# Expert lookup of a two-block network: a kept instruction order for VectorE and ScalarE, and another sharing of the gathered rows

## The chip, the cores and the metric

The kernel runs on one core of a Trainium2 chip. The metric is the device time of one execution in microseconds (us); lower is better. Engines are named as in the profile: PE (TensorE matmuls; PEld is its weight load), DVE (VectorE), ACT (ScalarE), POOL (GpSimd), SP (SyncE, which here only issues transfers).

## The reference

Two network blocks run one after the other on 512 tokens of width 1024 in float32. The change lies in one part of the first block, an expert layer: each token picks 16 of 16384 one-neuron experts for each of 8 heads, and the output is the weighted sum of the experts' rows of v.

```python
def block(xb):
    q = (xb @ wq).reshape(PEER_BLOCK, PEER_HEADS, 2, PEER_DKEY // 2)
    s1 = jnp.einsum('thd,hnd->thn', q[:, :, 0], keys[:, 0]).astype(f32)
    s2 = jnp.einsum('thd,hnd->thn', q[:, :, 1], keys[:, 1]).astype(f32)
    v1, i1 = lax.top_k(s1, PEER_TOPK)
    v2, i2 = lax.top_k(s2, PEER_TOPK)
    cand = (v1[..., :, None] + v2[..., None, :]).reshape(PEER_BLOCK, PEER_HEADS, PEER_TOPK * PEER_TOPK)
    sc, ci = lax.top_k(cand, PEER_TOPK)
    e = (jnp.take_along_axis(i1, ci // PEER_TOPK, axis=-1) * PEER_NKEYS
         + jnp.take_along_axis(i2, ci % PEER_TOPK, axis=-1))
    g = jax.nn.softmax(sc, axis=-1)
    hid = jnp.einsum('thkd,td->thk', u[e], xb).astype(f32)
    a = (jax.nn.gelu(hid, approximate=False) * g).astype(xb.dtype)
    return jnp.einsum('thk,thkd->td', a, v[e])
```

## The kernel before

The first 128 tokens gather their experts' rows; the other 384 take all 16384 experts densely and weigh the unchosen ones with zero. The layer runs in four stages, and PE works through all of them.

**Choice, with u sums beside it.** For each block of 128 tokens, `topk_block` picks the experts with chains of short DVE instructions (`top16`), a POOL sum and some one-hot comparisons. Meanwhile PE makes the u sums for the dense tokens: 64 pairs of 128 experts each (`hidden`), every pair in two pieces of weights. A piece comes in by SP as `raw` (512 KB), ACT rounds it to `whi` (L147), DVE makes the rest `wlo` (L149), and PE does 24 matmuls with them (L71, L72 with the high part of x, L76 with the low part). `wget` has the next two pieces split ahead. A finished pair goes through Gelu on ACT to `G` (L1250) and on to memory.

**Rows of u.** As soon as the first block has chosen, `Rows.step` runs among the rest: POOL gathers 128 rows of u (one for each of the first 128 tokens, 512 KB; four buffers), and DVE multiplies and sums them against the tokens (L1026). There are 128 such steps for u and later 128 for v (L1030).

**Build.** After the last choice, `build` makes the dense weights (expert x token), four tokens at a time, 96 groups: DVE writes two one-hot tiles (`hot`, L1208 and L1211), ACT scales one of them (L1210, four instructions), PE multiplies them (`aps`, L1227, two buffers), and ACT copies the result (L1228). They go to memory as `Ad`. The u sums go on beside it.

**v sums.** For each of the 128 blocks of experts: `gt` (the Gelu of the u sums, read back by ACT's queue) times `at` (the dense weights, read back four blocks at a time by POOL's queue, 768 KB, two buffers) on DVE (L1319), split into `ah` (ACT) and `al` (DVE, L289), and 24 matmuls with the block of v, whose weights come as `raw`, `whi` and `wlo` as above, into eight accumulators. About one row of v per block is gathered and added (L1030) among them.

A scheduler fixes the order of the instructions of each engine when the program is built; each engine then runs its list in that order and stops at any instruction whose inputs or buffers aren't ready. Two things in the text steer it. `pace` takes the u sums in quarters of a pair, and after each quarter lets `side` do work worth `SHARE / 2`, counted in the costs `T16`, `T256`, `TLK`, `BUILD` and `ROW`; `UPACE` says how many steps of `Rows` are owed for each unit of the other work. And `keep_in_program_order` pins single instructions behind what was written before them on their engine, among them the transfers of `at`.

Of the kernel before, what the change touches and what calls it, by code (L numbers as in the profile page):

```python
# [10 lines left out]
F32R = mybir.dt.float32r  # L11
U32 = mybir.dt.uint32
AF = mybir.ActivationFunctionType
ALU = mybir.AluOpType
# [4 lines left out]
P = 128  # L19
D = 1024  # L20
KT = 8
# [24 lines left out]
def r32(ap):  # L46
    return ap.bitcast(F32)


def mmx(nc, r, items, start, stop):  # L50


    rh, rl = r
    for out, (lh, ll) in items:
        nc.tensor.matmul(out, lh, rh, start=start, stop=False)  # L55
        nc.tensor.matmul(out, ll, rh, start=False, stop=False)  # L56
    for out, (lh, _) in items:
        nc.tensor.matmul(out, lh, rl, start=False, stop=stop)
# [54 lines left out]
def h_tiles(g):  # L113
    for k in range(KT):
        g.h[k] = g.res.tile([P, T], F32, tag=f"h{k}", name=f"h{k}")
# [7 lines left out]
def wsrc(g, name, idx):  # L123
    a = g.A[name]
    for i in idx:
        a = a[i]
    return a
# [14 lines left out]
def wload(g, raw, pool, hl):  # L142

    nc = g.nc
    _, a, b = raw.shape
    hi = pool.tile([P, a, b], F32R, tag="whi", name="whi", bufs=hl)
    nc.scalar.activation(hi, raw, AF.Copy)  # L147
    lo = pool.tile([P, a, b], F32R, tag="wlo", name="wlo", bufs=hl)
    nc.vector.tensor_tensor(lo, raw, r32(hi), op=ALU.subtract)  # L149
    return hi, lo  # L150
# [136 lines left out]
def split(g, t, hi, lo):  # L287
    g.nc.scalar.activation(hi, t, AF.Copy)  # L288
    g.nc.vector.tensor_tensor(lo, t, r32(hi), op=ALU.subtract)  # L289
# [647 lines left out]
NK = 128  # L937
TOPK = 16
FIRST = 4
LAST = 3  # L940
N1 = 122
PARTS = 4


GT = 128
RG = P // GT
NJ = P // RG
ND = S - GT
UG = 4

CH = 64
NCK = ND // CH

UH = 120

T16, T256, TLK, BUILD, ROW = 1.8, 2.55, 1.6, 1.3, 1.4
TOPKS = 16 * T16 + 3 + 8 * T256 + 8 * TLK + 2
BUILDS = NCK * (0.8 + CH // 4 * BUILD)
UPACE = UH * ROW / (3 * TOPKS + BUILDS)
SHARE = (4 * TOPKS + BUILDS + UH * ROW + 8) / N1  # L960


# [96 lines left out]
def peer_block(g, ni, tail):  # L1059

    tc, nc, A = g.tc, g.nc, g.A
    with ExitStack() as es:
# [7 lines left out]
        order = list(range(NK - FIRST, NK)) + list(range(NK - FIRST))  # L1070
        acc = Acc(g, es, "p_mm", 5).of(S)
        rg = Rows(g, es)
        g.third = rg.p

        with ExitStack() as e1:
# [105 lines left out]
            def tokens_last(b):  # L1181

                lists = picked[b]
                ps = pS.tile([P, 4, NK], F32, tag="S", name="lps")
                for i in range(3):
                    tc.keep_in_program_order(nc.tensor.transpose(ps[:, i], lists[:, i].rearrange("p a b -> p (a b)"), g.ident))
                lt = ip.tile([P, 3, P], F32, name=f"lt{b}")
                nc.scalar.activation(lt, ps[:, 0:3], AF.Copy)
                return lt
# [11 lines left out]
            def onehots(lt, t4):  # L1201

                o1, o2, oh = [hot[i].rearrange("p (t n) -> p t n", n=NK) for i in (t4 % 3, 3 + t4 % 2, 5 + t4 % 3)]

                def each(i):
                    return lt[:, i, 4 * t4:4 * t4 + 4].unsqueeze(2).to_broadcast([P, 4, NK])

                nc.vector.tensor_tensor(o2, io4, each(1), op=ALU.is_equal)  # L1208
                for j in range(4):
                    nc.scalar.activation(oh[:, j], o2[:, j], AF.Copy, scale=lt[:, 2, 4 * t4 + j:4 * t4 + j + 1])  # L1210
                nc.vector.tensor_tensor(o1, io4, each(0), op=ALU.is_equal)  # L1211
                return o1, oh

            def build(ab, c):

                b, t0 = divmod(GT + c * CH, P)
                lt = chosen[b]
                buf = ab.tile([P, NK, CH], F32, tag="ab", name="ab")
                nxt = [onehots(lt, t0 // 4), onehots(lt, t0 // 4 + 1)]
                yield 0.8  # L1220
                for t4 in range(CH // 4):
                    o1, oh = nxt.pop(0)
                    if t4 < CH // 4 - 2:
                        nxt.append(onehots(lt, t0 // 4 + t4 + 2))
                    ps = pA.tile([P, 4, NK], F32, tag="A", name="aps")
                    for j in range(4):
                        nc.tensor.matmul(ps[:, j], o1[:, j], oh[:, j], start=True, stop=True)  # L1227
                    nc.scalar.activation(buf[:, :, 4 * t4:4 * t4 + 4].rearrange("p i t -> p t i"), ps, AF.Copy)  # L1228
                    if out:
                        nc.scalar.dma_start(*out.pop(0))  # L1230
                    yield BUILD
                n = NK // (CH // 4)
                for i in range(0, NK, n):
                    out.append((Ad[c, :, i:i + n], buf[:, i:i + n]))

            def hidden(i, ts=None):

                at = {}

                def step(p):  # L1240
                    if p == 0:
                        at["acc"] = [acc.get(ND) for _ in range(2)]
                        at["gen"] = gemm2(g, [a[0] for a in at["acc"]], "peer_u", i, X)
                    for _ in range(8 // PARTS):
                        next(at["gen"])
                    if p < PARTS - 1:
                        return
                    gt = gp.tile([P, 2, ND], F32, tag="G", name="G") if ts is None else ts
                    for e in range(2):
                        nc.scalar.activation(gt[:, e], at["acc"][e][1], AF.Gelu)  # L1250
                    if ts is None:
                        nc.scalar.dma_start(Gd[i], gt)
                return [(lambda p=p: step(p)) for p in range(PARTS)]

            chosen, picked = {}, {}
            out = []

            def weights():

                for b in range(4):  # L1260
                    for n, c in enumerate(topk_block(b)):
                        yield c
                        if n == 12 and GT < b * P:
                            chosen[b - 1] = tokens_last(b - 1)
                for _ in range(8):
                    yield 1.0
                chosen[3] = tokens_last(3)
                e2.close()
                ab = e1.enter_context(tc.tile_pool(name="p_ab", bufs=2))
                for c in range(NCK):  # L1270
                    yield from build(ab, c)
                while out:
                    tc.keep_in_program_order(nc.gpsimd.dma_start(*out.pop(0)))

            def side():
                owed = 0.0
                for c in weights():
                    yield c
                    if rg.chosen:
                        owed += c * UPACE  # L1280
                        while owed > 0:
                            owed -= ROW
                            rg.step()
                            yield ROW
# [22 lines left out]
        def expert(n):  # L1307
            i = order[n]
            for m in range(n - n % 4, min(n + 5, NK), 4):
                if order[m] not in ats:  # L1310
                    ats[order[m]] = four_in(order[m])
            for m in range(n - n % 2, min(n + 4, NK), 2):
                if order[m] not in gts:
                    gts[order[m]] = two_in(order[m])
            return weighted(ats[i - i % 4][:, :, i % 4], gts[i - i % 2][:, i % 2])

        def weighted(at, gt):
            gv = gt.rearrange("p (c t) -> p c t", t=CH)
            nc.vector.tensor_tensor(gv, gv, at, op=ALU.mult)  # L1319
            ah = lp.tile([P, ND], F32R, tag="ah", name="ah")  # L1320
            al = lp.tile([P, ND], F32R, tag="al", name="al")
            split(g, gt, ah, al)
            return ah, al

        ats[NK - FIRST] = four_in(NK - FIRST)
        for i in range(NK - FIRST, NK, 2):
# [1 line left out]

        for i in range(N1 // 2, NK // 2):
            for m in hidden(i, gts.get(2 * i)):  # L1330
                m()
        h_tiles(g)
        tail.load(es)
        accs = [pp.tile([P, 512], F32, name=f"acc{k}") for k in range(3)] + [acc.get()[1] for _ in range(5)]
        rg.empty(accs, xh[0][:, 0:S])
        rg.due(NK - LAST)
        for n, i in enumerate(order[:-LAST]):
            a = expert(n)
            vh, vl = wget(g, "peer_v", i)
            mmx(nc, a, [(accs[k][:, GT:], (vh[:, k], vl[:, k])) for k in range(KT)], False, False)  # L1340
            rg.steps()
            if 8 <= n < 8 + KT:
                tc.keep_in_program_order(nc.sync.dma_start(g.h[n - 8][:, NM:], Hd[n - 8]))
        g.third = None

        last = [(expert(n), wload(g, wraw(g, wsrc(g, "peer_v", (order[n],))), lp, LAST)) for n in range(NK - LAST, NK)]
        for k in range(KT):
            for j, (a, (vh, vl)) in enumerate(last):
                mm3(nc, accs[k][:, GT:], (vh[:, k], vl[:, k]), a, False, False)
# [904 lines left out]
```

## Time and profile before

| What | Value |
|---|---|
| time, median of 3 runs | 3697.31 us (3693.34 to 3698.88) |
| profiled execution: time, span | 3703.12 us, 3701.4 us |
| mean granted clock of PE | 0.969 of full |
| busy share of the span: PE, DVE, ACT, POOL | 95%, 64%, 43%, 23% |
| rows of u begin, last choice ends | 679 us, about 971 us |
| build ends, v sums begin | 1303 us, 1335 us |
| v sums end, all but the last three blocks | 1943 us |

The span is that of one profiled execution, 1.7 us short of its own time. The busy time of PE is modelled from pipelined instructions, so it is a share of time with matmuls under way, not of peak speed. A granted clock of 1.00 is 2.4 GHz, 0.50 is 1.2 GHz, and a value between them is a mean over the stretch.

### The profile page before, as it was taken

The page shows a single profiled execution, that of the slowest core. Times are in us where ns is not written, and L with a number is a line of the kernel's source. Part 1 is how long each engine was busy: PE and PEld are TensorE (multiplying, and loading weights), DVE is VectorE, ACT ScalarE, POOL GpSimd, SP SyncE. Part 2 cuts the span into 40 slices and gives each one's busy share as a digit, 9 for nine tenths or more (in the row PEclk, how much of TensorE's full clock was granted, in tenths as well). Part 3 has the DMA queues.
Part 4 walks back from the last instruction along what each step waited for, and adds up shares of the span by engine and source line. Part 5 has one row for each costly group of instructions (what it writes and reads, how often), then busy time and mean ns, then how long its engine had stood idle before and what let it go on. Part 6 is the DMA issues. An engine that isn't in the chain of part 4 may idle for free. (4 is left out here: it accounts for less than half of the span.)

```text
span 3701.4 us, 56411 instructions
## 1 busy us (share of the span) xinstructions
PE 3510.0 (95%) x21979; PEld 3205.8 (87%) x21979; DVE 2381.2 (64%) x4395; ACT 1577.5 (43%) x2998; POOL 865.5 (23%) x828
## 2 busy tenths in 40 slices
PE   8999999899898888989989999999999999999999
PEld 6777888898898888889888899999999998877887
DVE  5764458899977756767677667767653336565333
ACT  4555333333498832333236444545432234443222
POOL 2431010444422134334433223222110003110000
PEclk9999999999999999999998889999999999999999
DMA  4223243777777788988882211111122222212232
GB/s 132 80 82 90 86 132 114 237 265 266 265 250 265 247 293 307 314 300 314 300 284 72 65 51 60 52 51 57 46 82 91 92 92 87 73 58 96 92 97 91
DMA packets 169492, 557.60 MB, mean 151 GB/s; under 512 B 19617, under 2 KB 20130, under 8 KB 169224
## 3 DMA queue, kind: packets, MB, share of 16 engines
q1 hardware_dynamic: 90228, 313.50, 25.6%
q0 software_dynamic: 49136, 170.64, 13.9%
q10 hardware_dynamic: 29860, 69.84, 5.3%
q8 instruction: 173, 2.83, 0.3%
q14 instruction: 95, 0.78, 0.1%
HBM read 492.20 MB, written 55.41 MB: 148 GB/s over the span
## 5 line engine op out<-in xcount | busy, mean ns | idle before, releaser
L72 PE MATMUL ps<-xh,wlo 128*128 128x264 f32 (+2 forms) x3296 | 1056.5, 332 | 61.0 <-DVE wlo L149 60.8
L71 PE MATMUL ps<-xh,whi 128*128 128x264 f32 (+2 forms) x3296 | 1073.2, 337 | 17.8 <-ACT xh L288 13.1
L147 ACT ACTIVATE whi<-raw 128x1024 fp32r<-128x1024 f32 x562 | 591.7, 1057 | 1010.2 <-PE ps L76 767.6
L149 DVE TENSOR_TENSOR wlo<-raw,whi 128x1024 fp32r<-128x1024 f32 x562 | 711.8, 1267 | 358.9 <-ACT whi L147 355.9
L76 PE MATMUL ps<-xl,whi 128*128 128x264 f32 (+2 forms) x3296 | 815.2, 332 | 6.6 <-DVE xl L289 6.5
L72 PEld LDWEIGHTS ps<-xh,wlo 128*128 128x128 f32 x3296 | 633.9, 193 | 103.6 <-DVE wlo L149 73.5
L71 PEld LDWEIGHTS ps<-xh,whi 128*128 128x128 f32 x3296 | 634.0, 193 | 55.8 <-ACT xh L288 15.4
L76 PEld LDWEIGHTS ps<-xl,whi 128*128 128x128 f32 x3296 | 566.5, 193 | 39.3 <-DVE xl L289 8.7
L1017 POOL DMA_INDIRECT row<-in_peer_v_dram,rix x128 | 202.1, 1579 | 369.4 <-DVE ro L1030 334.1
L1017 POOL DMA_INDIRECT row<-in_peer_ur_dram,rix x128 | 167.9, 1312 | 403.7 <-DVE row L1026 315.2
L71 PE MATMUL ps<-ah,whi 128*128 128x264 f32 (+1 forms) x768 | 230.1, 320 | 0.0
L72 PE MATMUL ps<-ah,wlo 128*128 128x264 f32 (+1 forms) x768 | 229.9, 320 | 0.0
L55 PE MATMUL ps<-ah,whi 128*128 128x384 f32 x640 | 224.5, 351 | 0.0
L56 PE MATMUL ps<-ah,wlo 128*128 128x384 f32 x640 | 223.4, 349 | 0.0
L288 ACT ACTIVATE ah<-gt 128x384 fp32r<-128x384 f32 x128 | 63.7, 524 | 323.5 <-DVE gt L1319 323.5
L56 PE MATMUL acc<-ah,wlo 128*128 128x384 f32 x384 | 138.6, 361 | 55.0 <-DVE wlo L149 54.8
L1319 DVE TENSOR_TENSOR gt<-gt,at 128x384 f32<-128x384 f32 x128 | 65.8, 553 | 187.3 <-DMA at<-Ad 178.5
L280 POOL TENSOR_TENSOR ssum<-ssum,sq 128x512 f32<-128x512 f32 (+1 forms) x49 | 75.7, 1550 | 456.5 <-ACT sq L279 456.1
L1026 DVE SCALAR_TENSOR_TENSOR row<-row,rx 128x1024 f32<-128x1024 f32 x128 | 168.0, 1313 | 6.6 <-DMA row<-in_peer_ur_dram,rix 6.6
L76 PE MATMUL ps<-al,whi 128*128 128x264 f32 (+1 forms) x768 | 163.2, 321 | 0.0
L1030 DVE SCALAR_TENSOR_TENSOR ro<-row,rhid,ro 128x1024 f32<-128x1024 f32 x127 | 162.4, 1279 | 0.0
L71 PEld LDWEIGHTS ps<-ah,whi 128*128 128x128 f32 x768 | 144.3, 188 | 11.3
(429 smaller groups left out, 6293.4 us busy)
## 6 DMA issues: line engine op xcount, KB each, us to landing
raw<-in_peer_u_dram SPq DMA_DIRECT2D x128, 512.0 KB
raw<-in_peer_v_dram SPq DMA_DIRECT2D x128, 512.0 KB
raw<-in_ff_up_dram SPq DMA_DIRECT2D x64, 512.0 KB
raw<-in_ff_down_dram SPq DMA_DIRECT2D x64, 512.0 KB
at<-Ad POOLq DMA_DIRECT2D x32, 768.0 KB
raw<-in_gdn_in_dram SPq DMA_DIRECT2D x48, 512.0 KB
Gd<-G ACTq DMA_DIRECT2D x62, 384.0 KB
gt<-Gd ACTq DMA_DIRECT2D x62, 384.0 KB
```

The costliest lines, as they stand in the source:

```text
L55: nc.tensor.matmul(out, lh, rh, start=start, stop=False)
L56: nc.tensor.matmul(out, ll, rh, start=False, stop=False)
L71: nc.tensor.matmul(segs[s][0], lh, xh[:, sl], start=start, stop=False)
L72: nc.tensor.matmul(segs[s][0], ll, xh[:, sl], start=False, stop=False)
L76: nc.tensor.matmul(segs[s][0], lh, xl[:, sl], start=False, stop=stop)
L147: nc.scalar.activation(hi, raw, AF.Copy)
L149: nc.vector.tensor_tensor(lo, raw, r32(hi), op=ALU.subtract)
L280: g.nc.gpsimd.tensor_tensor(self.t[:, 0:n], self.t[:, 0:n], sq[:, 0:n], op=ALU.add)
L1017: nc.gpsimd.indirect_dma_start(out=t, out_offset=None, in_=(self.U, self.V)[e], in_offset=bass.IndirectOffsetOnAxis(ap=self.ix[:, j:j + 1] ...
L1026: o = nc.vector.scalar_tensor_tensor(t, t, 1.0, self.x, op0=ALU.mult, op1=ALU.mult, accum_out=a)
L1030: o = nc.vector.scalar_tensor_tensor(self.o, t, a, self.o, op0=ALU.mult, op1=ALU.add)
L1319: nc.vector.tensor_tensor(gv, gv, at, op=ALU.mult)
```

## The change

From the end of the last choice to the end of the v sums, the scheduler no longer orders DVE and ACT: they keep the order in which the text is written (`manual_schedule`). The text is rearranged to suit:

- In the build, the copy of a group's result stands behind the four scalings of a later group (`last`), and the Gelu of a pair behind the first quarter of the next pair (`ends`).
- In the v sums, block n+2 is prepared while block n is multiplied (`AHEAD_V`): its product with `at` and its `ah` ahead of the row step, its `al` behind it.
- The 120 steps on rows of u that `side` hands out are shared as 44 in the choice and 76 in the build, where one pace served both before; and the costs of the choice's parts are set higher.

No instruction of DVE, ACT, PE or a transfer is added or taken away. Lines after L938 move down by 2 to 22.

```diff
+AHEAD_V = 2
...
-UH = 120
-
-T16, T256, TLK, BUILD, ROW = 1.8, 2.55, 1.6, 1.3, 1.4
+UH, UT = 120, 44
+
+T16, T256, TLK, BUILD, ROW = 2.2, 3.1, 2.0, 1.3, 1.4
 TOPKS = 16 * T16 + 3 + 8 * T256 + 8 * TLK + 2
 BUILDS = NCK * (0.8 + CH // 4 * BUILD)
-UPACE = UH * ROW / (3 * TOPKS + BUILDS)
+UPACE = [UT * ROW / (3 * TOPKS + 8), (UH - UT) * ROW / BUILDS]
 SHARE = (4 * TOPKS + BUILDS + UH * ROW + 8) / N1
...
+        kept, order_kept = es.enter_context(ExitStack()), []
...
                 nxt = [onehots(lt, t0 // 4), onehots(lt, t0 // 4 + 1)]
+                last = None
                 yield 0.8
...
-                    nc.scalar.activation(buf[:, :, 4 * t4:4 * t4 + 4].rearrange("p i t -> p t i"), ps, AF.Copy)
+                    if last is not None:
+                        last()
+                    last = lambda t4=t4, ps=ps: nc.scalar.activation(buf[:, :, 4 * t4:4 * t4 + 4].rearrange("p i t -> p t i"), ps, AF.Copy)
                     if out:
                         nc.scalar.dma_start(*out.pop(0))
                     yield BUILD
+                last()
...
                     for _ in range(8 // PARTS):
                         next(at["gen"])
-                    if p < PARTS - 1:
-                        return
+                    if p == 0 and ends:
+                        ends.pop(0)()
+                    if p == PARTS - 1:
+                        ends.append(end)
+
+                def end():
                     gt = gp.tile([P, 2, ND], F32, tag="G", name="G") if ts is None else ts
                     for e in range(2):
                         nc.scalar.activation(gt[:, e], at["acc"][e][1], AF.Gelu)
...
                 chosen[3] = tokens_last(3)
+                order_kept.append(kept.enter_context(tc.manual_schedule(engines={mybir.EngineType.DVE, mybir.EngineType.Activation})))
...
-                        owed += c * UPACE
+                        owed += c * UPACE[len(order_kept)]
...
-        def weighted(at, gt):
+            gt = gts[i - i % 2][:, i % 2]
             gv = gt.rearrange("p (c t) -> p c t", t=CH)
-            nc.vector.tensor_tensor(gv, gv, at, op=ALU.mult)
+            nc.vector.tensor_tensor(gv, gv, ats[i - i % 4][:, :, i % 4], op=ALU.mult)
             ah = lp.tile([P, ND], F32R, tag="ah", name="ah")
-            al = lp.tile([P, ND], F32R, tag="al", name="al")
-            split(g, gt, ah, al)
-            return ah, al
+            nc.scalar.activation(ah, gt, AF.Copy)
+
+            def lo():
+                al = lp.tile([P, ND], F32R, tag="al", name="al")
+                nc.vector.tensor_tensor(al, gt, r32(ah), op=ALU.subtract)
+                return ah, al
+            return lo
...
+        a = [expert(n)() for n in range(AHEAD_V)]
         for n, i in enumerate(order[:-LAST]):
-            a = expert(n)
             vh, vl = wget(g, "peer_v", i)
-            mmx(nc, a, [(accs[k][:, GT:], (vh[:, k], vl[:, k])) for k in range(KT)], False, False)
+            lo = expert(n + AHEAD_V) if n + AHEAD_V < NK else None
+            mmx(nc, a[n], [(accs[k][:, GT:], (vh[:, k], vl[:, k])) for k in range(KT)], False, False)
             rg.steps()
+            if lo is not None:
+                a.append(lo())
...
+        kept.close()
         g.third = None
```

On DVE these counts stand in the built orders (`wlo` pieces, steps on rows of u, one-hot tiles):

| Stretch of DVE's order | before | after |
|---|---|---|
| first choice block, before the first row step | 14 wlo | 15 wlo |
| first row step to the last second-level choice | 59 wlo, 68 rows, 8 hot | 52 wlo, 39 rows, 6 hot |
| from there to the last one-hot tile | 46 wlo, 54 rows, 184 hot | 52 wlo, 79 rows, 186 hot |

In the middle of the v sums DVE had two products of `gt` and `at` in a row, and two `al` in a row, of blocks close to the one that PE was at:

```order
L1319 TENSOR_TENSOR gt<-gt,at 128x384 x2
L149 TENSOR_TENSOR wlo<-raw,whi 128x1024
L1030 SCALAR_TENSOR_TENSOR ro<-row,rhid,ro 128x1024
L289 TENSOR_TENSOR al<-gt,ah 128x384 x2
L149 TENSOR_TENSOR wlo<-raw,whi 128x1024
L1030 SCALAR_TENSOR_TENSOR ro<-row,rhid,ro 128x1024
```

There it has now, for two blocks (`wlo`, `gt` and `al` of block n+2, `ro` in step n):

```order
L149 TENSOR_TENSOR wlo<-raw,whi 128x1024
L1331 TENSOR_TENSOR gt<-gt,at 128x384
L1032 SCALAR_TENSOR_TENSOR ro<-row,rhid,ro 128x1024
L1337 TENSOR_TENSOR al<-gt,ah 128x384
L149 TENSOR_TENSOR wlo<-raw,whi 128x1024
L1331 TENSOR_TENSOR gt<-gt,at 128x384
L1032 SCALAR_TENSOR_TENSOR ro<-row,rhid,ro 128x1024
L1337 TENSOR_TENSOR al<-gt,ah 128x384
```

The product with `at` stands two blocks ahead of PE now, and one block's work is a unit that repeats.

In the middle of the build, DVE's order before, with the tiles of a token block (`lt_8873`) and row steps between them:

```order
L1211 TENSOR_TENSOR hot<-iota,lt_8873 128x512
L149 TENSOR_TENSOR wlo<-raw,whi 128x1024
L1208 TENSOR_TENSOR hot<-iota,lt_8873 128x512
L1211 TENSOR_TENSOR hot<-iota,lt_8873 128x512
L149 TENSOR_TENSOR wlo<-raw,whi 128x1024
L1208 TENSOR_TENSOR hot<-iota,lt_8873 128x512
L1211 TENSOR_TENSOR hot<-iota,lt_8873 128x512
L1208 TENSOR_TENSOR hot<-iota,lt_8873 128x512
```

And at the same place now:

```order
L149 TENSOR_TENSOR wlo<-raw,whi 128x1024
L1212 TENSOR_TENSOR hot<-iota,lt_8611 128x512
L1215 TENSOR_TENSOR hot<-iota,lt_8611 128x512
L1028 SCALAR_TENSOR_TENSOR row,rhid<-row,rx 128x1024
L1212 TENSOR_TENSOR hot<-iota,lt_8611 128x512
L1215 TENSOR_TENSOR hot<-iota,lt_8611 128x512
L1028 SCALAR_TENSOR_TENSOR row,rhid<-row,rx 128x1024
L149 TENSOR_TENSOR wlo<-raw,whi 128x1024
```

A row step stands behind almost every group now, and a piece's `wlo` comes once in two groups.

## Rows read from the trace of the kernel before

**Rows 1.** The page's first part: busy time and share of the span of each engine
```profile
...
PE 3510.0 (95%) x21979; PEld 3205.8 (87%) x21979; DVE 2381.2 (64%) x4395; ACT 1577.5 (43%) x2998; POOL 865.5 (23%) x828
...
```

**Rows 2.** Windows by stage: PE, PEld, DVE, ACT, POOL busy (instructions), PE clock, DMA share, GB/s
```profile
...
679.00:971.00 292.00, 272.00 (x1502) 263.70 (x1502) 288.67 (x797) 102.15 (x151) 125.80 (x79) 0.96 0.80 269
971.00:1303.00 332.00, 296.36 (x1915) 289.40 (x1914) 253.09 (x363) 265.02 (x565) 85.82 (x60) 0.98 0.74 254
1303.00:1335.00 32.00, 22.34 (x116) 19.48 (x114) 8.37 (x9) 9.69 (x15) 14.31 (x26) 0.91 0.85 313
1335.00:1943.00 608.00, 551.34 (x3006) 540.81 (x3006) 421.14 (x516) 189.08 (x256) 229.21 (x159) 0.96 0.87 302
1943.00:3701.40 1758.40, 1706.83 (x12328) 1561.36 (x12328) 1006.86 (x1929) 711.85 (x1422) 269.05 (x335) 0.96 0.23 74
...
```

**Rows 3.** Waits of the v sums, 1335 to 1943: total, times, longest us
```profile
...
DVE gt L1319 <- DMA at<-Ad: 178.5, 30, 7.8
...
PE acc L56 <- DVE wlo L149: 54.8, 24, 4.6
...
```

**Rows 4.** Timeline of one expert group of the v sums: start, us, engine, line
```profile
...
1606.15 1.02 DVE L1319 TENSOR_TENSOR gt<-gt,at 128x384 f32<-128x384 f32 x2
...
1609.12 0.89 POOL L1294 DMA_DIRECT2D at<-Ad  x1
...
1611.49 1.28 DVE L1030 SCALAR_TENSOR_TENSOR ro<-row,rhid,ro 128x1024 f32<-128x1024 f32 x1
...
1613.18 0.19 PEld L55 LDWEIGHTS acc<-ah,whi 128*128 128x128 f32 x1
...
1617.34 0.19 PEld L55 LDWEIGHTS acc<-ah,whi 128*128 128x128 f32 x1
...
1619.99 1.03 DVE L1319 TENSOR_TENSOR gt<-gt,at 128x384 f32<-128x384 f32 x2 [7.22 <-DMA at<-Ad]
...
1620.94 1.22 DVE L149 TENSOR_TENSOR wlo<-raw,whi 128x1024 fp32r<-128x1024 f32 x1
...
1622.07 1.28 DVE L1030 SCALAR_TENSOR_TENSOR ro<-row,rhid,ro 128x1024 f32<-128x1024 f32 x1
1622.20 0.19 PEld L56 LDWEIGHTS acc<-ah,wlo 128*128 128x128 f32 x1 [4.68 <-DVE wlo L149]
...
1623.27 1.02 DVE L289 TENSOR_TENSOR al<-gt,ah 128x384 fp32r<-128x384 f32 x2
...
1624.20 1.22 DVE L149 TENSOR_TENSOR wlo<-raw,whi 128x1024 fp32r<-128x1024 f32 x1
...
```

**Rows 5.** Windows of 5 us in the v sums, columns as in Rows 2
```profile
...
1615.00:1620.00 5.00, 2.85 (x17) 2.53 (x15) 0.01 (x1) 0.00 (x0) 0.00 (x0) 1.00 1.01 383
1620.00:1625.00 5.00, 2.79 (x9) 2.79 (x10) 5.00 (x7) 2.88 (x4) 1.01 (x1) 0.75 0.64 222
...
```

**Rows 6.** Groups of instructions, 679 to 971, shapes apart
```profile
...
L72 PE MATMUL ps<-xh,wlo 128*128 128x384 f32 x472 | 163.8, 347 | 20.0 <-DVE wlo L149 19.9
...
L1026 DVE SCALAR_TENSOR_TENSOR row<-row,rx 128x1024 f32<-128x1024 f32 x68 | 93.9, 1382 | 5.6 <-DMA row<-in_peer_ur_dram,rix 5.6
...
L149 DVE TENSOR_TENSOR wlo<-raw,whi 128x1024 fp32r<-128x1024 f32 x59 | 79.4, 1346 | 0.0
...
```

**Rows 7.** Timeline at the end of the build: matmuls of one group of four tokens
```profile
...
1303.11 1.03 PEld L1227 LDWEIGHTS aps<-hot 128*128 128x128 f32 x8
...
```

**Rows 8.** Groups of instructions, 971 to 1303, shapes apart
```profile
...
L72 PE MATMUL ps<-xh,wlo 128*128 128x384 f32 x384 | 131.4, 351 | 33.8 <-DVE wlo L149 33.7
...
L1228 ACT ACTIVATE ab<-aps 128x512 f32<-128x512 f32 x95 | 102.8, 1083 | 19.4 <-PE aps L1227 17.6 <-issue 1.7
...
L1026 DVE SCALAR_TENSOR_TENSOR row<-row,rx 128x1024 f32<-128x1024 f32 x56 | 69.2, 1236 | 1.0 <-DMA row<-in_peer_ur_dram,rix 1.0
L1211 DVE TENSOR_TENSOR hot<-iota,lt 128x512 f32<-128x512 f32 x93 | 64.2, 690 | 65.5 <-PE aps L1227 64.5 <-issue 0.7
...
L147 ACT ACTIVATE whi<-raw 128x1024 fp32r<-128x1024 f32 x46 | 48.9, 1066 | 18.2 <-PE ps L76 10.9 <-DMA raw<-in_peer_u_dram 7.3
...
```

More of the change, by code (lines that the diff above doesn't have):

```diff
@@ L1253, in hidden @@
                 return [(lambda p=p: step(p)) for p in range(PARTS)]
+            ends = []
             chosen, picked = {}, {}
@@ L1314, in expert @@
                     gts[order[m]] = two_in(order[m])
-            return weighted(ats[i - i % 4][:, :, i % 4], gts[i - i % 2][:, i % 2])
-        def weighted(at, gt):
+            gt = gts[i - i % 2][:, i % 2]
             gv = gt.rearrange("p (c t) -> p c t", t=CH)
-            nc.vector.tensor_tensor(gv, gv, at, op=ALU.mult)
+            nc.vector.tensor_tensor(gv, gv, ats[i - i % 4][:, :, i % 4], op=ALU.mult)
             ah = lp.tile([P, ND], F32R, tag="ah", name="ah")
-            al = lp.tile([P, ND], F32R, tag="al", name="al")
-            split(g, gt, ah, al)
-            return ah, al
+            nc.scalar.activation(ah, gt, AF.Copy)
[4 more added lines that the diff above has]
+            return lo
         ats[NK - FIRST] = four_in(NK - FIRST)
@@ L1331, in peer_block @@
                 m()
+        while ends:
+            ends.pop(0)()
         h_tiles(g)
@@ L1336, in peer_block @@
         rg.due(NK - LAST)
+        a = [expert(n)() for n in range(AHEAD_V)]
         for n, i in enumerate(order[:-LAST]):
-            a = expert(n)
             vh, vl = wget(g, "peer_v", i)
-            mmx(nc, a, [(accs[k][:, GT:], (vh[:, k], vl[:, k])) for k in range(KT)], False, False)
+            lo = expert(n + AHEAD_V) if n + AHEAD_V < NK else None
+            mmx(nc, a[n], [(accs[k][:, GT:], (vh[:, k], vl[:, k])) for k in range(KT)], False, False)
             rg.steps()
+            if lo is not None:
+                a.append(lo())
             if 8 <= n < 8 + KT:
                 tc.keep_in_program_order(nc.sync.dma_start(g.h[n - 8][:, NM:], Hd[n - 8]))
+        kept.close()
         g.third = None
-        last = [(expert(n), wload(g, wraw(g, wsrc(g, "peer_v", (order[n],))), lp, LAST)) for n in range(NK - LAST, NK)]
+        last = [(a[n] if n < len(a) else expert(n)(), wload(g, wraw(g, wsrc(g, "peer_v", (order[n],))), lp, LAST)) for n in range(NK - LAST, NK)]
         for k in range(KT):
```

## The prediction

> **What bounds the kernel now.** The first part of the page gives PE 95% of the span, so the windows by stage come next: in each, what would PE need if it never waited, and what does it take? One block of the v sums is 24 matmuls, and from its first weight load to the next block's first there are 1617.34 - 1613.18 = 4.16 us where PE runs freely [rows 1, 4]. A u piece has 24 matmuls of the same shape, and a build group takes 1.03 us [rows 7]. This makes a floor for each stage, and what the stage takes beyond it is its excess.
>
> - Choice from the first row step on, 679 to 971: 472 / 8 = 59 pieces [rows 6] are 245 us, and the 1502 - 59 x 24 = 86 other matmuls, at the build's 1.03 / 8 us each, 11. Floor 256, taken 292 [rows 2], excess 36.
> - Build, 971 to 1303: 384 / 8 = 48 pieces [rows 8] are 200 us, 95 groups 98. Floor 298, taken 332, excess 34, nearly all of it PE waiting for `wlo` (33.7 us, [rows 8]).
> - v sums, 1335 to 1943: 3006 / 24 = 125 blocks, floor 521, taken 608 [rows 2], excess 87. PE is idle for 608 - 551 = 57 us, 54.8 of them behind `wlo` [rows 3]. The mean granted clock of 0.96 costs another 4% of 608 = 24 us; the rest is modelled ends.
>
> So 157 us lie above PE's floor here. What puts them there differs. In the choice it is load: DVE is busy 288.67 of 292 us [rows 2]. In the v sums it is order, and the timeline shows it: the last products with a group of four blocks' `at` start at 1606.15, the next group's transfer is issued only at 1609.12 (POOL's list has row gathers ahead of it), DVE is through with its other work at 1612.8, and stands until 1619.99, 10.9 us after the issue [rows 4]. The `wlo` that PE needs is behind that product, and PE stands for 4.7 us. Its clock then is granted at 0.75 for the next 5 us, part of them on the 1.2 GHz level [rows 5]. DVE waits like that 30 times, once for each group of `at`, 178.5 us in all [rows 3].
>
> **Rows of u moved out of the choice.** The built orders have 39 row steps there for 68, and 52 pieces for 59. An instruction of DVE holds it for some 0.08 us less than its duration: `wlo` lasts 1.22 us and the next one starts after 1.13, a row step of v 1.28 and 1.20 [rows 4]. So 29 row steps at 1.382 - 0.08 = 1.30 us [rows 6] are 38 us, 7 `wlo` at 1.346 - 0.09 are 9, two one-hot tiles at 0.6 are 1. DVE's need falls from 289 to 241 us. PE's floor for 52 pieces and the same other matmuls is 216 + 11 = 227. DVE is still the longer of the two, so the stretch takes 241 to 250; at 245 the excess falls from 36 to 18. **Gain 18**, between 5 (the handing over between two nearly full engines costs as much as it does now) and 30 (PE at its floor but for a few us).
>
> **The same rows in the build, in kept order.** 25 row steps at about 1.24 us [rows 8] are 31 us, 6 more `wlo` 7: DVE needs 253 + 38 = 291. ACT has 6 more roundings of 1.07 us [rows 8] and the Gelus of three pairs, which I put at half of that: 265 + 9 = 274. PE's floor is 54 pieces and 95 groups, 225 + 98 = 323. So PE stays the longest, and the added rows lie beside it. Transfers: 254 GB/s over 332 us are 84 MB; 25 gathers and 6 pieces of 512 KB add 16, so 100 MB at about 295 GB/s, which is below what the v sums move now (302, [rows 2]). What the order gives back is not in a row: DVE's waits of 65.5 us for a free one-hot tile [rows 8] stay, since they are set by three buffers, but `wlo` is written two pieces ahead of its use, 8.3 us, and every piece behind two groups. The excess can go from 34 to about 3, or stay. I take 18, the middle. **Gain 16**, 0 to 31; a loss is a rival below.
>
> The later copy and the later Gelu cost nothing as long as their buffers have room. A Gelu a quarter of a pair (2.1 us) later holds two of five accumulators; the pair after next wants them 8.3 us after the end of the first. The copy stands behind four scalings, and PE needs its buffer two groups on; a group comes every 332 / 95 = 3.5 us. Without that cover it is the rival.
>
> **The v sums in a pipeline.** DVE's unit per block is `wlo` 1.13, product 0.47, 1.06 row steps at 1.20 and `al` 0.47, all start to start [rows 4]: 3.34 us of 4.16. It can't run away from PE: `wlo` of block n+2 takes the buffer of n-1, so DVE starts a block's unit when PE starts block n, two blocks or 8.3 us ahead of use. Now the transfer of `at`. Its buffer is free after the last product of the group before the one in use, done in step 4g-3; its first product is in step 4g+2. That is five steps, 20.8 us, less up to 3 us that POOL may take for a gather ahead of it (here the issue came 2 us after the product), against the 10.9 us that it takes now [rows 4]. So DVE's wait goes, and with it PE's 54.8 us and most of the missing clock. What may be late next are transfers as such: 302 GB/s over 608 us are 184 MB, and at a share of 0.87 the same mix could move at most 302 / 0.87 = 347 GB/s, or 530 us, a little above PE's 521. In single 5 us stretches 383 GB/s were moved [rows 5], so 347 is no wall. I take an excess of 35 us: 556 us, 331 GB/s, share 0.95. **Gain 52**, between 17 (591 us, transfers late) and 75 (533 us).
>
> A rule bears on this term. The Trainium skill (DMA: Bandwidth & Descriptors, Where 436 GB/s comes from) says that transfers between HBM and SBUF are bound by HBM at about 358 GB/s a core. By that figure, an estimate, 184 MB need 514 us, PE would be the bound and the term nearer 65, for 3600 us in all; a stretch of [rows 5] went above the figure, so I hold to the rows.
>
> **Edges.** From 1303 to 1335 PE is busy for 22 of 32 us [rows 2]: the last dense weights are written and the first `at` read back, as before. From 1943 on (1758 us) the text is unchanged. Zero for both, 5 us either way.
>
> **Sum.** 18 + 16 + 52 = 86 us. The profiled execution took 3703.1 us (span 3701.4), and would take 3617; it lies 5.8 us above the median of the runs, so the median goes from 3697.3 to 3611.
>
> **Rivals.**
> - *Transfers bind the v sums.* For it: a share of 0.87 already, and row gathers of both stages come more evenly but not fewer. `at` then lands later than 18 us, or `raw` does. Gains 17 + 18 + 12 = 47: 3650. Against it: the stretch with 383 GB/s.
> - *All three stages near PE's floor.* Gains 28 + 29 + 72 = 129: 3568. For it: no engine's need is above PE's in build and v sums. Against: DVE at 241 of 227 in the choice.
> - *The kept order stalls the build: slower.* ACT waits at a copy for PE (17.6 us now, [rows 8]); in a kept list the next scalings wait behind it, PE's next group waits for them, and once PE is late for one group the list can't be turned round. Today PE waits 0.36 us a group (34 / 95). If that becomes 2 us, the build loses 95 x 1.64 = 156 us in place of gaining 16; with 70 gained elsewhere, 86 slower: 3783. It decides from (34 + 70) / 95 = 1.1 us a group. Against it: ACT needs 274 of 323 us, and two groups of lead.
> - *The change doesn't do what it says.* DVE's lead is 8.3 us, less 2.7 to the end of the product, 5.6. If `at` came as late as now (7.2 us), PE would still stand for 1.6 us a group of four, where its mean is 54.8 / 30 = 1.8 now: 7 us gained there and 34 in the other stages, 3656. Against it: the five steps counted above.
>
> **How the numbers follow.** The forecast (3585 to 3635) has 0.55, transfers binding or `at` still late (3635 to 3690) 0.23, all near the floor 0.13, the stalled build 0.06, no change to speak of 0.03. The range takes the forecast, nearly all of the second case and the upper part of the third: 3572 to 3675. A measurement of this kernel tells a change of 0.2%, 7.4 us, from none. Faster by that: 0.55 + 0.23 + 0.13 = 0.91; the same 0.03; slower 0.06.
>
> **What would show it.** In the profile after: no DVE wait for `at` worth naming and PE's wait for `wlo` in the v sums under 15 us; that stage at 540 to 575 us, clock 0.98 or more, DMA share 0.92 to 0.97. In the choice DVE still above 95% busy, the stretch some 245 us. In the build PE's idle time under 20 us with DVE near 85% and ACT near 80%. Wrong would be: waits of `whi` for `raw` in the v sums of more than 30 us (transfers); PE waiting for ACT's copy or scalings by tens of us in the build (the order).

## The result and the profile after

The changed kernel takes 3634.41 us (median of 4 runs, 3628.02 to 3642.98), the kernel before 3695.77 on the same chip: a ratio of 0.9835, 95% interval [0.9809, 0.9861], 61 us faster. The forecast was 3611, in a range of 3572 to 3675. The total lies near, but the terms that make it don't: one has the wrong sign.

Windows of the changed kernel, one for each stage, columns as in [rows 2]. The bounds are events here and in all windows of stages below: the first row step, the end of the last choice, the last copy of the build, the first and the last matmul of the v sums.

```profile
680.30:940.90 260.60, 243.35 (x1348) 233.63 (x1347) 256.47 (x742) 92.23 (x137) 81.61 (x50) 0.97 0.69 225
940.90:1327.60 386.70, 338.91 (x2033) 307.01 (x2032) 286.80 (x416) 274.75 (x575) 102.57 (x84) 0.98 0.80 261
1327.60:1360.10 32.50, 24.30 (x126) 22.68 (x124) 9.13 (x11) 10.91 (x17) 16.90 (x28) 0.89 0.91 339
1360.10:1896.70 536.60, 534.92 (x3084) 533.84 (x3085) 445.86 (x538) 208.36 (x266) 173.23 (x166) 1.00 0.95 348
1896.70:3626.25 1729.55, 1677.19 (x12252) 1532.57 (x12250) 992.98 (x1914) 703.98 (x1410) 262.86 (x332) 0.97 0.23 74
```

The same windows of the kernel before:

```profile
678.70:971.90 293.20, 273.20 (x1508) 264.89 (x1508) 289.87 (x799) 102.86 (x152) 125.80 (x79) 0.97 0.80 270
971.90:1304.40 332.50, 296.86 (x1921) 289.87 (x1919) 252.19 (x361) 264.61 (x565) 85.82 (x60) 0.98 0.74 255
1335.10:1959.60 624.50, 567.40 (x3084) 556.40 (x3085) 435.07 (x533) 197.21 (x267) 235.32 (x164) 0.95 0.86 296
1959.60:3701.35 1741.75, 1690.77 (x12252) 1545.78 (x12250) 992.83 (x1912) 703.62 (x1409) 262.84 (x331) 0.97 0.23 74
```

With the floors of the prediction (4.16 us for 24 matmuls, 1.03 for a build group, 11 us for the choice's other matmuls) the excess over PE's floor is:

| Stage | before | forecast | after |
|---|---|---|---|
| choice | 36 | 18 | 261 - (52.6 pieces: 219 + 11) = 31 |
| build | 34 | 18 | 387 - (52.7 pieces and 96 groups: 219 + 99) = 69 |
| v sums | 87 (90 by these bounds) | 35 | 537 - (128.5 blocks: 535) = 2 |

By lengths: the v sums are 88 us shorter, the choice 32.6 (28 of it are the 6.7 pieces that it no longer holds), the build is 54 longer (19 of it are the 4.7 pieces that it holds more; the other two moved into the stretches ahead of the choice and behind the build), and the stretch behind the v sums is 12 shorter with the same instructions. The profiled executions differ by 75 us, the medians by 61: after's profiled execution lies 6 below its median, before's 7 above.

Waits in the v sums after, 1360 to 1888, as in [rows 3] (waiting engine and releaser, us in total, times, longest us): first three of DVE and ACT, then all of PE.

```profile
...
ACT ah L1333 <- DVE gt L1331: 227.4, 126, 4.0
...
DVE wlo L149 <- ACT whi L147: 86.0, 109, 2.0
...
ACT whi L147 <- DMA raw<-in_peer_v_dram: 12.3, 7, 3.1
...
```
```profile
PE acc L55 <- ACT ah L1333: 1.2, 2, 0.7
PE acc L58 <- DVE al L1337: 0.9, 1, 0.9
```

DVE's 178.5 us behind `at` and PE's 54.8 us behind `wlo` [rows 3] are gone. The waits that are left are those of engines that are ahead of PE. Waits in the build after, 941 to 1327, and two of before, 971 to 1303:

```profile
...
DVE wlo L149 <- ACT whi L147: 95.5, 44, 3.4
ACT hot L1214 <- DVE hot L1212: 82.4, 41, 3.1
PEld aps L1232 <- ACT ab L1235: 41.9, 62, 2.6
...
PE ps L72 <- DVE wlo L149: 23.0, 33, 6.3
PE aps L1232 <- ACT ab L1235: 22.7, 40, 2.3
...
```
```profile
...
ACT hot L1210 <- DVE hot L1208: 16.2, 16, 2.6
...
DVE wlo L149 <- ACT whi L147: 6.1, 6, 1.6
...
```

Here no engine is full: PE 88%, DVE 74%, ACT 71%. DVE waits for ACT, ACT for DVE, and PE for both; before, the first two waits were 6.1 and 16.2 us. DVE's waits for a free one-hot tile (64.5 us, [rows 8]), which I had said would stay, are down to 0.8 us. Timeline of DVE, ACT and PE through one turn (start, us; idle time before and its releaser in brackets):

```profile
1166.12 1.22 DVE L149 TENSOR_TENSOR wlo<-raw,whi 128x1024 fp32r<-128x1024 f32 x1 [3.23 <-DMA Ad<-ab]
...
1168.41 0.69 DVE L1212 TENSOR_TENSOR hot<-iota,lt 128x512 f32<-128x512 f32 x1
...
1174.61 1.23 DVE L149 TENSOR_TENSOR wlo<-raw,whi 128x1024 fp32r<-128x1024 f32 x1 [2.56 <-ACT whi L147]
```
```profile
1165.03 1.06 ACT L147 ACTIVATE whi<-raw 128x1024 fp32r<-128x1024 f32 x1
1169.19 0.70 ACT L1214 ACTIVATE hot<-hot,lt 128x128 f32<-128x128 f32 x2 [3.10 <-DVE hot L1212]
...
1172.72 1.00 ACT L1235 ACTIVATE ab<-aps 128x512 f32<-128x512 f32 x1
1173.54 1.04 ACT L147 ACTIVATE whi<-raw 128x1024 fp32r<-128x1024 f32 x1
```
```profile
1167.40 0.62 PE L72 MATMUL ps<-xh,wlo 128*128 128x384 f32 x2 [0.60 <-DVE wlo L149]
...
1173.78 1.16 PE L1232 MATMUL aps<-hot 128*128 128x128 f32 x8 [0.94 <-ACT ab L1235]
```

The first line names a transfer as the releaser, but the `whi` that this `wlo` reads ended on ACT at 1166.09, 0.03 us before it started. `wlo`, a row step and the tile to be scaled take DVE from 1166.12 to 1169.1; only then can ACT start eight scalings and two copies, and only behind those, at 1173.54, stands the `whi` that DVE's next `wlo` waits for: 1174.61 - 1166.12 = 8.5 us a turn with one piece and two groups, for which PE needs 4.16 + 2 x 1.03 = 6.2. This turn is one of the longer ones: the 30 turns of the build with one piece and two groups take 6.5 to 8.6 us, 7.9 on average. PE takes this `wlo` the moment it is written: nothing is left of the lead of two pieces.

### The profile page after: what moved, and what is told of

It reads as the page before. It is cut to its first block, busy times and chain, and to the rows that moved or that the text cites. A ratio compares the mean times of both kernels' runs of the same rounds, so it can differ in the third digit from the quotient of the medians.

```text
span 3626.3 us, 56462 instructions
## 1 busy us (share of the span) xinstructions
PE 3483.1 (96%) x21979; PEld 3164.9 (87%) x21979; DVE 2399.4 (66%) x4395; ACT 1591.4 (44%) x2998; POOL 776.2 (21%) x828
## 5 line engine op out<-in xcount | busy, mean ns | idle before, releaser
L1019 POOL DMA_INDIRECT row<-in_peer_ur_dram,rix x128 | 146.1, 1142 | 465.7 <-DVE row L1028 372.1
L55 PE MATMUL ps<-ah,whi 128*128 128x384 f32 x640 | 215.5, 337 | 0.0
L56 PE MATMUL ps<-ah,wlo 128*128 128x384 f32 x640 | 215.1, 336 | 0.0
L1019 POOL DMA_INDIRECT row<-in_peer_v_dram,rix x128 | 138.1, 1079 | 276.9 <-DVE ro L1032 261.5
L1214 ACT ACTIVATE hot<-hot,lt 128x128 f32<-128x128 f32 x384 | 122.0, 390 | 93.3 <-DVE hot L1212 89.6
L72 PEld LDWEIGHTS ps<-ah,wlo 128*128 128x128 f32 x768 | 144.3, 188 | 10.9
```

The lines of the kernel that those rows point to most:

```text
L72: nc.tensor.matmul(segs[s][0], ll, xh[:, sl], start=False, stop=False)
L1019: nc.gpsimd.indirect_dma_start(out=t, out_offset=None, in_=(self.U, self.V)[e], in_offset=bass.IndirectOffsetOnAxis(ap=self.ix[:, j:j + 1] ...
```

## The experiments

**What is held against what.** Theory A: in the build, the order of the text gives ACT no lead. The tile that it scales stands on DVE behind a `wlo` that itself waits for ACT, so the two take turns, and kept order leaves nobody to put it otherwise. Theory B: the rows moved into the build cost that time, by DVE's load and their transfers. For the v sums: the gain comes from the kept order, from the rearranged text, or from the rows. Ratios are to the kernel before on the same chip.

**Kept order in the v sums alone.** The text and the rows' shares stay as changed; the scheduler orders choice and build.

```diff
-                order_kept.append(kept.enter_context(tc.manual_schedule(engines={mybir.EngineType.DVE, mybir.EngineType.Activation})))
+                order_kept.append(None)
...
+        kept.enter_context(tc.manual_schedule(engines={mybir.EngineType.DVE, mybir.EngineType.Activation}))
         a = [expert(n)() for n in range(AHEAD_V)]
```

> The kept order begins at the v sums; choice and build are left to the scheduler, rows shared 44 and 76 as in the changed kernel. Theory A (in the kept order ACT and DVE take turns in the build, each waiting for the other, some 45 us): the build falls from 386 to 335-350 us, ACT's waits for the one-hot tile from 82 to under 30 us, v sums stay at 525-535, 3585-3600 us in all. Theory B (the 25 row steps moved into the build are what it pays for): the build stays above 370 us, 3620-3640 in all.

3607.21 us, ratio 0.9737 [0.9707, 0.9768]. Windows of its build and v sums:

```profile
941.70:1294.50 352.80, 320.05 (x2032) 312.38 (x2031) 288.52 (x418) 275.35 (x574) 116.62 (x85) 0.98 0.82 287
1326.90:1867.20 540.30, 538.28 (x3084) 537.18 (x3085) 446.72 (x538) 208.41 (x266) 175.36 (x166) 0.99 0.94 346
```

With the same rows and as many matmuls the build is 34 us shorter, its excess (35) is that of before, and ACT waits for the one-hot tile for 15 us. Build, v sums and total lie 3 to 7 us above the ranges of A, build and total below those of B. That speaks for A.

**One pace for the rows, as before, and kept order.** Costs and pace of the kernel before in the changed one.

```diff
-T16, T256, TLK, BUILD, ROW = 2.2, 3.1, 2.0, 1.3, 1.4
+T16, T256, TLK, BUILD, ROW = 1.8, 2.55, 1.6, 1.3, 1.4
...
-UPACE = [UT * ROW / (3 * TOPKS + 8), (UH - UT) * ROW / BUILDS]
+UPACE = [UH * ROW / (3 * TOPKS + BUILDS)] * 2
```

> The changed kernel with the costs and the one pace of before: some 68 row steps in the choice and 54 in the build, kept order everywhere it was kept. Theory A: the build still has an excess of 45 us or more over PE's floor of about 298, so 340-360 us, the choice is back at 285-295; 3620-3640 in all, no gain. Theory B: the build is back near 332 us with an excess of 34, 3600-3615 in all.

3647.78 us, ratio 0.9845 [0.9818, 0.9872]. Window of its build:

```profile
967.70:1333.50 365.80, 318.37 (x1923) 285.76 (x1922) 251.44 (x363) 262.48 (x563) 76.95 (x60) 1.00 0.71 230
```

48 pieces as in the kernel before, DVE busy for 251 of 366 us, and an excess of 67: the loss is there without the rows. A again. The ratio can't be told from the changed kernel's 0.9835: with the build kept in order, the other sharing of the rows gained nothing that the time shows.

**The new share of rows alone.** The kernel before with `UPACE` by phase and the new costs; nothing is kept, no text rearranged.

```diff
...
-                        owed += c * UPACE
+                        owed += c * UPACE[3 in chosen]
```

> The kernel before with the new costs and the sharing of rows by phase alone: no kept order, no pipeline. Theory A: choice near 261 us, build 335-350, v sums near 608 as before; 3680-3695 in all, a small gain or none. Theory B: the build grows to 370 us or more without any kept order, 3710-3730, slower than before.

3686.69 us, ratio 0.9943 [0.9924, 0.9962]. Windows of its build and v sums:

```profile
941.00:1290.60 349.60, 317.98 (x2024) 311.35 (x2023) 285.89 (x414) 274.16 (x576) 115.38 (x85) 0.97 0.84 287
1325.00:1953.30 628.30, 569.66 (x3084) 559.24 (x3085) 439.06 (x539) 196.88 (x267) 245.38 (x166) 0.95 0.85 297
```

The build takes the rows at an excess of 33: theory B falls. The shares alone are worth 0.6%, and nothing in the v sums.

**The tile to be scaled, one group ahead.** The changed kernel; DVE writes `o2` of a group before `o1` of the group ahead of it. Same instructions, same buffers.

```diff
+            def second(lt, t4):
+                o2 = hot[3 + t4 % 2].rearrange("p (t n) -> p t n", n=NK)
+                nc.vector.tensor_tensor(o2, io4, lt[:, 1, 4 * t4:4 * t4 + 4].unsqueeze(2).to_broadcast([P, 4, NK]), op=ALU.is_equal)
...
-                nc.vector.tensor_tensor(o2, io4, each(1), op=ALU.is_equal)
...
                         nxt.append(onehots(lt, t0 // 4 + t4 + 2))
+                        if t4 < CH // 4 - 3:
+                            second(lt, t0 // 4 + t4 + 3)
```

> The changed kernel, but DVE writes the one-hot tile that ACT scales one group earlier in the text, so that ACT's scalings find it ready; same instructions and buffers. Theory A: ACT's waits for that tile fall from 82 to under 20 us, PE's waits for ACT's copy from 23 to under 8, the build to 335-355 us, 3585-3605 in all. Theory B: ACT waits less, but the build stays above 370 us.

3588.54 us, ratio 0.9686 [0.9657, 0.9715]. Window and waits of its build:

```profile
937.70:1274.00 336.30, 320.68 (x2033) 305.60 (x2032) 286.09 (x416) 274.49 (x575) 107.97 (x84) 0.99 0.88 299
```
```profile
...
DVE wlo L149 <- ACT whi L147: 38.3, 38, 2.6
...
ACT hot L1217 <- DVE hot L1207: 16.9, 22, 2.5
...
PE ps L72 <- DVE wlo L149: 11.7, 12, 6.3
...
```

ACT's wait for the tile falls from 82 to 17 us, PE's for ACT's copy from 23 to 2, the turns with one piece and two groups to 6.6 us on average, and the build by 50 to an excess of 18: one link of the turn is taken out and the loss is gone. That settles A, and in a kept order the build is now better than the scheduler's (353 us with the same rows, in the run told first). Whether another link, such as the copy that stands behind a later group's scalings, would have done as well was not run.

**The rearranged text alone.** The changed kernel with the scheduler everywhere.

```diff
-                order_kept.append(kept.enter_context(tc.manual_schedule(engines={mybir.EngineType.DVE, mybir.EngineType.Activation})))
+                order_kept.append(None)
```

> The changed kernel with its rearranged text, but with the scheduler ordering DVE and ACT everywhere, as before. Theory A (the kept order, not the rearranged text, makes engines take turns in the build): the build is back near 352 us, as in the run that kept the order in the v sums alone. For the v sums there are two theories. If the text's rearrangement carries the gain (a block prepared two blocks ahead), the v sums stay near 540 us, and the kernel comes to about 3607 us, ratio 0.974. If the kept order carries it, the scheduler again puts the products early in DVE's list, DVE waits for the tile of dense weights as before, and the v sums are at 600 us or more, the kernel at 3665 or more, ratio 0.99.

3697.51 us, ratio 0.9992 [0.9973, 1.0012]. Window and waits of its v sums:

```profile
1321.70:1943.30 621.60, 557.35 (x3083) 539.79 (x3084) 436.76 (x533) 192.93 (x260) 216.24 (x163) 0.98 0.84 301
```
```profile
...
DVE gt L1331 <- DMA gt<-Gd: 176.2, 54, 5.7
...
PE acc L56 <- DVE wlo L149: 63.9, 48, 3.7
...
```

The build is back at 353 us. The v sums lose all but 3 us of their gain, so the gain needs the kept order, and the text alone does not give it. The late transfer is another one now (`gt`, which ACT's list issues), as long in sum as `at` was before.

**One block ahead in place of two,** on top of the tile a group ahead.

```diff
-AHEAD_V = 2
+AHEAD_V = 1
```

> The kernel with the one-hot tile a group ahead, and the v sums' pipeline one block deep in place of two. My prediction's count of steps says that the dense weights land in time by three steps or more; if so, one block of lead (4.16 us) is as good as two, PE waits for the chain product, rounding, rest no more than now, and the v sums stay at 535 to 545 us, ratio 0.969. If the lead is what hides late transfers or ACT's and DVE's handing over, PE waits some us a group and the stage goes to 560 us or more, ratio 0.975 or above.

3596.43 us, ratio 0.9706 [0.9674, 0.9737]; the v sums 538.1 us beside 538.3. One block of lead does as well, so it is not the second block of depth that gives the gain. With the run before, what is left is the kept order, in which every product, and with it every transfer that waits for a buffer, comes once a block. The text of before in kept order, without any lead, was not run, so whether the order needs a lead of one block stays open.

**32 rows in the choice,** on top of the tile a group ahead.

```diff
-UH, UT = 120, 44
+UH, UT = 120, 32
```

> The kernel with the one-hot tile a group ahead, and 32 rows of u handed out in the choice, 88 in the build, for 44 and 76. If DVE's load alone makes the excess of the choice (31 us over PE's floor, DVE 98% busy) and the build, now near its floor, takes the rows beside PE, the choice loses about 16 us of DVE work with 2 or 3 pieces moved along: 243 to 248 us; the build gains two or three pieces and grows by 10 to 14 to about 349, and the sum of both falls by 3 to 8 us, ratio about 0.967. If the build's DVE can't take 12 rows more without making PE wait, the sum stays or grows by 5 to 10 us, ratio 0.970 or above.

3579.05 us, ratio 0.9661 [0.9629, 0.9693]. Windows of its choice and build:

```profile
677.70:923.60 245.90, 229.95 (x1284) 221.75 (x1283) 238.91 (x720) 89.80 (x134) 71.04 (x40) 0.97 0.63 210
923.60:1263.50 339.90, 329.42 (x2109) 318.42 (x2109) 299.55 (x439) 279.68 (x580) 123.81 (x95) 0.99 0.91 316
```

Choice and build together take 585.8 us for 258.9 + 336.3 = 595.2 without the edit. The ratios overlap, so the time alone doesn't show the 9 us; the stages do.

**The choice's products on DVE,** on top of the tile a group ahead. Theory C: DVE's instructions are stretched beside POOL's. Timelines of DVE and POOL in the choice of the changed kernel:

```profile
851.07 3.44 DVE L1154 TENSOR_TENSOR cand<-cf,iota 128x1024 f32<-128x1024 f32 x1
...
855.57 1.21 DVE L1159 TENSOR_REDUCE lists<-cand 128x64 f32<-128x1024 f32 x1
```
```profile
850.19 3.24 POOL L1156 TENSOR_TENSOR cand<-cand,ixf 128x1024 f32<-128x1024 f32 x1 [0.82 <-DVE cand L1154]
854.59 3.27 POOL L1156 TENSOR_TENSOR cand<-cand,ixf 128x1024 f32<-128x1024 f32 x1 [1.16 <-DVE cand L1154]
```

```diff
-                    nc.gpsimd.tensor_tensor(sel[:, hs], sel[:, hs], ixf...
+                    nc.vector.tensor_tensor(sel[:, hs], sel[:, hs], ixf...
```

> The kernel with the one-hot tile a group ahead, and the choice's eight products of 128x1024, which POOL makes, made by DVE. Theory C (DVE's instructions are stretched while POOL works on a large tensor, which ate 8 us of the choice's gain): the eight comparisons (`cand`) fall from 2.05 to about 1.21 us each and the splits from 1.42 to below 1.37 on average, so DVE's work grows by 8 x 1.2 less about 9 us, nearly nothing, and the choice stays within 3 us of 259. If the stretch has another cause (PE, transfers, the rows), the means stay as they are and the choice grows by some 9 us to 268.

3574.25 us, ratio 0.9636 [0.9602, 0.967]. Window of its choice, and the comparisons on DVE from the span's start to 950 us (16, those of all four choice blocks):

```profile
674.90:928.50 253.60, 243.88 (x1367) 236.05 (x1366) 250.21 (x737) 95.14 (x141) 61.27 (x44) 0.98 0.71 237
```
```profile
L1154 DVE TENSOR_TENSOR cand<-cf,iota 128x1024 f32<-128x1024 f32 x16 | 19.6, 1224 | 0.1
```

DVE does eight instructions more and the choice is 5 us shorter. The comparison is back at 1.22 us, and the splits of the choice last 1.342 us in place of 1.416: theory C holds.

**Products and 32 rows; then the sums on DVE too.** Two kernels on one chip: the kernel just told with 32 rows, and that with its sums (L1135) moved too.

```diff
-UH, UT = 120, 44
+UH, UT = 120, 32
```
```diff
-                nc.gpsimd.tensor_tensor(cand, v[:, 0:8].unsqueeze(3).to_broadcast([P, 8, TOPK, TOPK]),
+                nc.vector.tensor_tensor(cand, v[:, 0:8].unsqueeze(3).to_broadcast([P, 8, TOPK, TOPK]),
```

> The kernel with the one-hot tile a group ahead and the products on DVE, and 32 rows of u handed out in the choice, 88 in the build. Its parts alone gave ratios of 0.9686 (tile), 0.9636 (tile and products) and 0.9661 (tile and 32 rows). If the two edits add up (each takes DVE work out of the choice, which DVE bounds), choice and build together fall from 583 to about 577 us and the ratio is 0.962. If the choice is then bound by PE at its floor, they overlap, and the ratio stays at 0.9636.

> The kernel before this one, with the choice's four sums of 128x2048 moved from POOL to DVE too. POOL takes 3.7 us for one, DVE would take some 2.4, by twice a 128x1024 tensor's 1.21. If POOL's work on large tensors stretches DVE's by as much as it seemed with the products (the eight products moved at no cost, and 5 us less), DVE gains about as much as it takes on, and the choice is the same within 3 us, ratio within 0.002 of the kernel before this one. If the sums disturb nobody (DVE then runs short instructions on 128x128), the choice grows by 3 x 2.4 = 7 us.

3565.91 us, ratio 0.9656 [0.9642, 0.9671], and 3554.37 us, ratio 0.9611 [0.9595, 0.9627]. For the first, the ratio misses the 0.962 of two edits that add up and can't be told from the products' alone, though its choice and build are 10 us shorter together (236.4 + 337.3 for 253.6 + 329.8); why the time doesn't show them stays open. The second is faster than the first by more than its forecast (0.0045 in the ratio, 4 us in the choice), and the fastest of all. Windows of the second's choice and build, and its splits and row steps in the choice:

```profile
673.00:905.00 232.00, 226.47 (x1298) 220.23 (x1297) 231.17 (x716) 89.38 (x133) 37.40 (x29) 1.00 0.71 229
905.00:1237.10 332.10, 324.17 (x2080) 313.46 (x2079) 295.78 (x441) 278.94 (x578) 113.94 (x91) 0.99 0.92 320
```
```profile
L149 DVE TENSOR_TENSOR wlo<-raw,whi 128x1024 fp32r<-128x1024 f32 x51 | 61.8, 1211 | 0.0
L1028 DVE SCALAR_TENSOR_TENSOR row<-row,rx 128x1024 f32<-128x1024 f32 x29 | 35.1, 1211 | 1.7 <-DMA row<-in_peer_ur_dram,rix 1.7
...
```

With nothing but row gathers left on POOL there, split and row step both last 1.211 us; with the sums still on POOL, in the first kernel, they lasted 1.309 and 1.327. The build, 54.7 pieces and 96 groups, is 6 us above its floor of 227 + 99.

## Why the prediction was right in sum and wrong in two terms

The median lies in the range, but partly by luck. Build and v sums both came out beyond the bounds that I had given their terms, on opposite sides: against the forecast of 86 us the build is 51 worse and the choice 13, the v sums are 36 better, and 17 came from stretches that I had put at zero, which makes 75 in the profiled executions.

**v sums: right mechanism, term too small (52, measured 85 to 88).** `at` is in time and PE's wait is gone, as the count of steps said, and the clock is granted at 1.00. The mis-sized part is the excess of 35 us that I left for late transfers. The cap of 347 GB/s, from 302 at a share of 0.87, accounts for 9 of it (530 us less 521); the other 26 had no row behind them. Two windows of 100 us within the v sums of the changed kernel:

```profile
1360.00:1460.00 100.00, 99.88 (x576) 99.88 (x577) 82.15 (x107) 38.66 (x51) 29.94 (x31) 1.00 0.99 368
1460.00:1560.00 100.00, 100.00 (x579) 100.00 (x578) 83.17 (x100) 38.12 (x48) 33.47 (x32) 1.00 0.98 357
```

The transfers do run at a share of 0.98 to 0.99, but at 357 to 368 GB/s, and PE is never kept waiting for them. PE's floor is the bound, 2 us away. The Trainium skill's figure of about 358 GB/s (DMA: Bandwidth & Descriptors, Where 436 GB/s comes from) was nearer than my cap, and by it the term would have been 65; one window went above it, by 10.

**Build: wrong sign (gain 16 forecast, loss of 35).** The step that failed is "PE stays the longest, and the added rows lie beside it", with the leads behind it: `wlo` "two pieces ahead of its use, 8.3 us, and every piece behind two groups". I compared each engine's load with PE's need. Loads were right (DVE 287 us for 291 forecast, ACT 275 for 274), but in two kept lists that hand work to each other the length of a turn counts, 7.9 us for 6.2 of PE. A lead of two pieces covers a single delay; where the turns are longer than PE's need, it is used up and doesn't come back. My rival with the stalled build had the effect right, PE waiting for ACT's copy, but not its cause: it had ACT standing at a copy for PE, and that wait fell from 17.6 to 1.1 us; ACT stood for DVE's tile, and DVE for ACT's `whi`. Its size stayed below the point of decision, 69 us on 96 groups or 0.7 us a group, where it would have decided from 1.1, so the kernel is faster all the same.

**Choice: right direction, too large (gain 18, measured 5).** Groups of DVE in the choice after, 680 to 941, as in [rows 6], and the comparisons of before, 679 to 971:

```profile
L149 DVE TENSOR_TENSOR wlo<-raw,whi 128x1024 fp32r<-128x1024 f32 x52 | 73.6, 1416 | 0.1
L1028 DVE SCALAR_TENSOR_TENSOR row<-row,rx 128x1024 f32<-128x1024 f32 x39 | 53.7, 1377 | 6.2 <-DMA row<-in_peer_ur_dram,rix 6.2
L1154 DVE TENSOR_TENSOR cand<-cf,iota 128x1024 f32<-128x1024 f32 x8 | 16.4, 2045 | 0.1
...
```
```profile
L1150 DVE TENSOR_TENSOR cand<-cf,iota 128x1024 f32<-128x1024 f32 x8 | 9.6, 1214 | 0.0
```

The counts of rows and pieces held (52 and 39); DVE's need was to fall to 241 us and fell to 256. Of these 15 us, the eight `cand` comparisons took 6.6 (1.214 to 2.045 us each), and 52 splits at 1.416 in place of 1.346 another 3.6; the rest is not assigned. I had priced the instructions that stay at their durations of before, though POOL stretches those that come to stand beside its products, and the new order put three of the eight comparisons there (3.40 to 3.44 us each). Against the 1.211 us without tensor work on POOL, after's choice holds 8 x 0.83 + 52 x 0.205 + 39 x 0.166 = 24 us of stretch. Before, the row steps and splits held 68 x 0.171 + 59 x 0.135 = 20 us of it. POOL's eight products and three sums are the same in both, and moving rows away did not take a share of the stretch along, as my prices had it. The share of "above 95%" was right at 98%.

**Edges: forecast 0.** The stretch behind the v sums gave 12 us in the profiled execution with the same 12252 matmuls. It took from 1730 to 1754 us in the twelve profiled kernels, one execution of each, with the kernel before at 1742 in their midst, so nothing shows it to be an effect of the change. Taken together: 5 - 35 + 88 + 12 = 70, and 5 from the stretches ahead of the choice and behind the build, which hold two u pieces more (8.3 us) and are 3.4 us longer; that makes the 75 us of the profiled executions, 61 by the medians.

**Of what would show it:** no wait for `at`, PE's wait for `wlo` and a share of 0.92 to 0.97 came true, and the waits of `whi` for `raw` stayed at 12 us. The stage at 537 is below my 540 to 575, the choice at 261 above my 245; in the build PE was idle for 48 us and not under 20, with DVE at 74% for 85% and ACT at 71% for 80%, and PE waiting for ACT's copy by tens of us was the sign that I had named for the order being wrong.

## What to carry to other kernels

When an order is kept by hand, add up one turn across the engines that feed each other (here `wlo`, row, tile, scalings, copies, `whi`), and not only each engine's load: where the turn is longer than what the bounding engine needs, move one producer a step ahead, which here cost no instruction and gave 50 us. Keep the order only where it pays, stage by stage: kept order gave 81 to 85 us in the v sums and, with that producer unmoved, took 34 in the build. Moving work between two engines that disturb each other can be worth it even towards the fuller one.

## What the runs showed of the hardware

- A DVE instruction that reads two tensors stood still while POOL worked on a tensor: started at 851.07 within a POOL product that ended at 853.43, it ended at 854.51, 1.1 us later, where its like take 1.2 us in all. The profile shows this as a longer instruction and not as a wait. The reduction at 855.57, which reads one tensor, took its 1.21 us within the next product. The Trainium skill (SBUF — State Buffer, Who interferes with whom) says this: a DVE instruction with two inputs in SBUF contends with a GpSimd instruction that reads SBUF, by an exclusive lock, and a DVE instruction with at most one input in SBUF doesn't, outside the modes that use two ports. The trace agrees, and I had not drawn on it.
- Transfers ran at a share of 0.98 to 0.99 and 357 to 368 GB/s in four windows of 100 us in a row, 1360 to 1760 us of the changed kernel, while PE was busy for all but 0.1 us at a granted clock of 1.00.
